# Reading the moving columns of fp32r products last to first, and moving the weight tiles by steps of 32 bytes

## The chip, the cores and the metric

The kernel runs on one core of a Trainium2 chip. The time is the device time of one execution in microseconds (us); a version is judged by its median over several executions. The profile comes from one execution of its own.

## The reference

Two transformer blocks follow each other on 256 tokens of width 2048, all in float32. The first has banded attention and gated linear attention, the second block attention and retention; each then has a gated feed-forward part of width 5632 and a gated embedding. Nearly all the arithmetic is in products with large weight matrices:

```python
def first_block(x, p, ...):
    h = rms_norm(x, norm_mix_w);  proj = h @ w_in                    # 2048 x 6160
    ...                                                              # attention, gated linear attention
    x = x + concat([y_a, y_g]) @ w_out                               # 2048 x 2048
    u = causal_depthwise_conv(rms_norm(x, norm_ffn_w) @ w_ffn_up)    # 2048 x 11264
    x = x + (gelu(u_gate) * u_val) @ w_ffn_down                      # 5632 x 2048
    x = x + sigmoid(rms_norm(x, norm_ple_w) @ w_ple_gate) * (p @ w_ple_proj)
    return rms_norm(x, final_norm_w)
# second_block: w_in_2 2048 x 7168, w_o_2, w_gate_2 and w_up_2 2048 x 5632, w_down_2, w_ple_gate_2, w_ple_proj_2
```

## The kernel before

**Products in parts.** Each float32 operand is split into a high part, rounded to fp32r by a copy, and a low part, the rest. A product is made of three: high times high, high times low and low times high. `weight_plan` (line 29) cuts all weights into 880 tiles of 128 partitions x up to 1024 numbers, in the order in which they are used. Tiles follow each other in *chunks*, the tiles that belong to the same output columns.

**Narrow chunks** (`prod_b`, line 276): 256 output columns, four k-steps in a tile, 4, 5 or 6 tiles in a chunk. The weights stand still (128 x 128) and the activations move. For each k-step and each half `b` of the output there is a pair of products: the high weights against 512 columns (high and low part of the activations, side by side), and the low weights against the 256 columns of the high part. The plan has 172 narrow chunks: 140 of 4 tiles, 16 of 6 and 16 of 5, together 736 tiles, and a tile has 8 pairs.

**Wide chunks** (`prod_a`, line 289): up to 512 output columns, two k-steps in a tile, 8 tiles in a chunk. Here the activations stand still and the weights move: 12 products a tile. The plan has 17 of them: 15 are 512 columns wide, the second is 256 and the third 272. Eight further tiles, the embedding's, go through `prod_p` (line 267), 24 products of 256 columns each.

**Where a weight tile lies.** `load` (line 178) fetches a tile by DMA seven tiles ahead, ScalarE writes its high part four ahead (`split_hi`, line 188), VectorE its low part three ahead (`split_lo`, line 196). Each of the two parts has its own buffers of 4096 + 256 bytes, aligned to 256 bytes, and `split_tile` (line 170) chooses how many bytes into the buffer the part begins. `PARTS_AT` gives this for the high and the low part: `narrow` 192 and 0, `lead` 0 and 32, `wide` 0 and 0. `plan_kind` calls the first two tiles of every eighth narrow chunk (n mod 8 = 0) and the first tile where n mod 8 = 4 `lead`: 65 tiles in all. The activations lie in regions aligned to 256 bytes.

**Order.** The order of the instructions is written out by hand: a tile's `slot` (line 207) issues the splits and the load for later tiles and a step of the pending evictions and side work, then come the products of the tile. All matmuls of these kinds go through `mm` (line 259), so the profile shows them on line 260, and the accumulators are called `acc`. Two accumulators of two PSUM banks alternate.

Of the kernel before, what the change touches and what calls it, by code (L numbers as in the profile page):

```python
# [13 lines left out]
T = 256  # L14
# [7 lines left out]
HALVES = ((0, 24), (24, 44))  # L22
LINE = 256
SCRATCH = 2048
LEADS = {0: 2, 4: 1}
PARTS_AT = {"narrow": (192, 0), "lead": (0, 32), "wide": (0, 0)}


def weight_plan():

    tiles = []
    full = tuple(range(KT))

    def gemm(n, kts, chunks):
        for ch in chunks:
            for i in range(0, len(kts), n):  # L40
                tiles.append((kts[i : i + n], ch))

    def even(name, lo, hi, step):
        return [[(name, c, c + step)] for c in range(lo, hi, step)]

    def wide(name, lo, hi):
        gemm(2, full, even(name, lo, hi, 512))

    def narrow(name, lo, hi, kts=full):
        gemm(4, kts, even(name, lo, hi, 256))  # L50

    def ffn(gate, up, off, down):
        for a, b in HALVES:
            gemm(4, full, [[(gate, c * P, c * P + P), (up, off + c * P, off + c * P + P)] for c in range(a, b)])
            narrow(down, 0, D, tuple(range(a, b)))

    def ple(gate, proj):
        for c in range(0, D, 512):
            narrow(gate, c, c + 512)
            gemm(2, (0, 1), even(proj, c, c + 512, 512))  # L60

    gemm(2, full, [[("w_in", 4096, 4608)], [("w_in", 4608, 4864)], [("w_in", 4864, 5120), ("w_in", 6144, 6160)]])
    narrow("w_in", 3072, 4096)
    narrow("w_in", 0, 2048)
    wide("w_in", 2048, 3072)
    wide("w_in", 5120, 6144)
    narrow("w_out", 0, D, MIX_ORDER)
    ffn("w_ffn_up", "w_ffn_up", FF, "w_ffn_down")
    ple("w_ple_gate", "w_ple_proj")
    wide("w_in_2", 0, 3072)  # L70
    narrow("w_in_2", 3072, 5120)
    wide("w_in_2", 5120, 7168)
    narrow("w_o_2", 0, D)
    ffn("w_gate_2", "w_up_2", 0, "w_down_2")
    ple("w_ple_gate_2", "w_ple_proj_2")
    return tiles


def plan_offsets(tiles):
    out, off = [], 0  # L80
    for kts, ch in tiles:
        f = len(kts) * sum(b - a for _, a, b in ch)
        out.append((off, f))
        off += P * f
    return out, off


def plan_kind(tiles):

    out, last, n, k = [], None, -1, 0  # L90
    for kts, ch in tiles:
        if ch != last:
            n, k = n + (len(kts) == 4), 0
        out.append("wide" if len(kts) == 2 else "lead" if k < LEADS.get(n % 8, 0) else "narrow")
        k += 1
        last = ch
    return out

# [15 lines left out]
class Net:  # L114
# [4 lines left out]
    def __init__(self, nc, tc, pools, ins, out):  # L119
        self.nc, self.tc = nc, tc  # L120
        self.sp, self.wp, self.ps = pools
        self.ins, self.out = ins, out
        self.plan = weight_plan()
        self.offs, _ = plan_offsets(self.plan)
        self.kind = plan_kind(self.plan)
        self.i = 0
        self.raw, self.H, self.L = {}, {}, {}
        self.ev, self.side = [], []
        self.done = set()
        self.nacc = 0  # L130
        self.forced = []
        self.sizes = {}
        self.off = SCRATCH + 128
        self.pad(self.wp)
        self.off += 4 * 4096 + 9 * (4096 + LINE)
# [32 lines left out]


    def split_tile(self, i, tag, bufs):  # L170
        o = PARTS_AT[self.kind[i]][tag == "wl"] // 4
        return self.wp.tile([P, 1024 + LINE // 4], F32R, tag=tag, name=tag, bufs=bufs)[:, o : o + 1024]

    def cut(self, i, part):
# [101 lines left out]
    def prod_b(self, acts, acc):  # L276
        nk = len(acts)
        for g in range(0, nk, 4):
            self.need_acts(acts[g : g + 4])
            H, L, w = self.slot(4)  # L280
            assert w == 256
            for j in range(4):
                x, _ = acts[g + j]
                for b in range(2):
                    sl = slice(j * w + b * P, j * w + b * P + P)
                    self.mm(acc[:, b, :], H[:, sl], x, g + j == 0, False)
                    self.mm(acc[:, b, T:], L[:, sl], x[:, :T], False, g + j == nk - 1)

    def prod_a(self, acts, acc):
        nk = len(acts)  # L290
        for g in range(0, nk, 2):
            self.need_acts(acts[g : g + 2])
            H, L, w = self.slot(2)
            for j in range(2):
                x, _ = acts[g + j]
                for t in range(2):
                    o = acc[:, t, :w]
                    hs = slice(t * P, t * P + P)
                    ls = slice(T + t * P, T + t * P + P)
                    sl = slice(j * w, j * w + w)  # L300
                    self.mm(o, x[:, hs], H[:, sl], g + j == 0, False)
                    self.mm(o, x[:, hs], L[:, sl], False, False)
                    self.mm(o, x[:, ls], H[:, sl], False, g + j == nk - 1)

    def join(self, acc, dst):

# [1113 lines left out]
```

## Time and profile before

| what | value |
|---|---|
| median of 3 runs | 2477.26 us (2477.2 to 2477.84) |
| profiled execution | 2477.44 us, its span 2475.6 us |
| TensorE busy | 2464.0 us, 14162 matmuls |
| VectorE, ScalarE busy | 1667.6 us, 1279.5 us |
| read from HBM | 464.80 MB, 189 GB/s over the span |

A matmul's row gives its start, and a modelled length that overlaps the next matmul. What a product costs is therefore read from the distance between starts. A weight load stands beside the product before it, on a row of its own (PEld). In the timeline `acc<-f,wh` is a product of the activations `f` with the high part of a weight tile, `acc<-f,wl` with the low part.

### The profile page before, as it was taken

The numbers are of one execution on the slowest core, as the hardware profiler recorded it, in microseconds if no ns is written. First come the engines' busy times: TensorE is split into PE (matmuls) and PEld (weight loads), VectorE is DVE, ScalarE is ACT, GpSimd is POOL, SyncE is SP. The second block draws the span as 40 slices with busy tenths as digits, with TensorE's granted clock in tenths as the row PEclk, the third lists the DMA queues.
The fourth block names the chain that finished last, engine by engine and source line by source line (L and its number), as shares of the span: only waits on it lengthen the run. The fifth ranks groups of instructions, "written<-read, shape, count | busy, mean of one in ns | idle before, by whom it ended". The sixth has DMA issues, their size and how long they took to land.

```text
span 2475.6 us, 36486 instructions
## 1 busy us (share of the span) xinstructions
PE 2464.0 (100%) x14162; PEld 2153.4 (87%) x14162; DVE 1667.6 (67%) x2374; ACT 1279.5 (52%) x1713; POOL 8.4 (0%) x60
## 2 busy tenths in 40 slices
PE   9999999999999999999999999999999999999999
PEld 7888788888888888888888888888888888888888
DVE  6666667777755787767886765676666556666665
ACT  6545655665633565545644644555554434554453
POOL 0000000000000000000000000000000000000000
PEclk9999999999999999999999999999999999999999
DMA  7545455555555555555555455555555555555554
GB/s 245 190 145 192 155 190 188 195 194 192 193 195 192 192 195 195 195 199 192 198 179 187 162 183 188 182 193 191 195 192 192 195 195 193 191 195 198 191 201 147
DMA packets 133550, 469.30 MB, mean 190 GB/s; under 512 B 14960, under 2 KB 17392, under 8 KB 133376
## 3 DMA queue, kind: packets, MB, share of 16 engines
q1 hardware_dynamic: 133232, 466.95, 56.5%
q8 instruction: 111, 1.82, 0.3%
q14 instruction: 63, 0.52, 0.1%
q10 hardware_dynamic: 144, 0.01, 0.0%
HBM read 464.80 MB, written 2.10 MB: 189 GB/s over the span
## 4 chain that ended last, share of the span: by engine, by line
PE 99%; DMA 0%; DVE 0%; ACT 0%; issue 0%; SPq 0%; ACTq 0%
PE acc L260 95%; PE sc L260 2%; PE pv L260 1%; PE tr L698 0%; DMA raw<-weights 0%; PE sc L1147 0%; ACT wh L194 0%; PE sc L1230 0%; PE sc L566 0%; DVE ty L996 0%; SPq L428 0%; DVE wl L205 0%; DVE X L997 0%; PE tr L785 0%; SPq L186 0%
## 5 line engine op out<-in xcount | busy, mean ns | idle before, releaser
L205 DVE TENSOR_TENSOR wl<-raw,wh 128x1024 fp32r<-128x1024 f32 (+1 forms) x881 | 1069.0, 1214 | 761.8 <-PE acc L260 492.9
L194 ACT ACTIVATE wh<-raw 128x1024 fp32r<-128x1024 f32 (+1 forms) x881 | 925.6, 1051 | 844.9 <-PE acc L260 665.6
L260 PE MATMUL acc<-f,wh 128*128 128x512 f32 x2816 | 960.0, 390 | 0.0
L260 PE MATMUL acc<-f,wl 128*128 128x256 f32 x2816 | 777.7, 276 | 0.0
L260 PEld LDWEIGHTS acc<-f,wh 128*128 128x128 f32 x2816 | 528.6, 188 | 110.5
L260 PEld LDWEIGHTS acc<-f,wl 128*128 128x128 f32 x2816 | 528.6, 188 | 0.0
L260 PE MATMUL acc<-g,wh 128*128 128x512 f32 x1408 | 479.6, 389 | 0.0
L260 PE MATMUL acc<-g,wl 128*128 128x256 f32 x1408 | 388.8, 276 | 0.0
L260 PEld LDWEIGHTS acc<-g,wh 128*128 128x128 f32 x1408 | 264.3, 188 | 55.5
L260 PEld LDWEIGHTS acc<-g,wl 128*128 128x128 f32 x1408 | 264.3, 188 | 0.0
L260 PE MATMUL acc<-hp,wh 128*128 128x512 f32 x512 | 175.5, 390 | 0.0
L260 PE MATMUL acc<-hp,wl 128*128 128x256 f32 x512 | 141.5, 276 | 0.0
L260 PEld LDWEIGHTS acc<-hp,wh 128*128 128x128 f32 x512 | 96.1, 188 | 19.9
L260 PE MATMUL acc<-wh,m2b 128*128 128x512 f32 x320 | 102.8, 393 | 0.0
L260 PE MATMUL acc<-wh,m2a 128*128 128x512 f32 x320 | 102.3, 392 | 0.0
L260 PEld LDWEIGHTS acc<-hp,wl 128*128 128x128 f32 x512 | 96.1, 188 | 0.0
L897 ACT ACTIVATE ty<-tU,vec 128x256 f32<-128x256 f32 x88 | 48.3, 596 | 74.4 <-DVE tU L893 74.4
L308 ACT ACTIVATE tq<-acc 128x512 f32<-128x512 f32 x124 | 71.8, 579 | 4.7 <-PE acc L260 4.7
L260 PE MATMUL acc<-wh,h0a 128*128 128x512 f32 (+2 forms) x224 | 67.1, 376 | 4.7 <-ACT wh L194 4.7
L260 PEld LDWEIGHTS acc<-wh,m2a 128*128 128x128 f32 x320 | 60.1, 188 | 12.3
L260 PEld LDWEIGHTS acc<-wh,m2b 128*128 128x128 f32 x320 | 60.1, 188 | 12.2
L260 PE MATMUL acc<-h0a,wh 128*128 128x512 f32 x192 | 67.6, 395 | 0.0
(272 smaller groups left out, 2746.9 us busy)
## 6 DMA issues: line engine op xcount, KB each, us to landing
raw<-weights SPq DMA_DIRECT2D x863, 512.0 KB, 3.3
raw<-weights SPq DMA_DIRECT2D x10, 256.0 KB, 3.3
raw<-weights SPq DMA_DIRECT2D x8, 272.0 KB, 2.8
aB<-bias SPq DMA_DIRECT2D x8, 256.0 KB, 3.5
X<-xT SPq DMA_DIRECT2D x7, 256.0 KB, 7.1
dk<-decay SPq DMA_DIRECT2D x8, 192.0 KB, 3.7
out<-X SPq DMA_DIRECT2D x6, 256.0 KB, 2.8
pr<-pT SPq DMA_DIRECT2D x2, 256.0 KB, 4.9
```

The costliest lines, as they stand in the source:

```text
L194: self.nc.scalar.activation(self.H[i][:, a], self.raw[i][:, a], AF.Copy)
L205: self.nc.vector.tensor_sub(self.L[i][:, a], r[:, a], self.H[i][:, a].bitcast(F32))
L260: self.nc.tensor.matmul(out, lhsT, rhs, start=start, stop=stop, skip_group_check=True, **kw)
L308: self.nc.scalar.activation(m, acc[:, :, T:], AF.Copy)
L897: nc.scalar.activation(y[:, b, :], u[:, b, 0:T], AF.Identity, scale=self.col("cw0", j), bias=self.col("b_ffn_conv", j))
```

## The change

The table of places with its three kinds goes. A narrow tile's high part now begins 32 x (n mod 8) bytes into its buffer and its low part 32 x ((n // 8 + n) mod 8), with n the number of the narrow chunk; wide tiles stay at 0 and 0. In narrow chunks both products of a pair take their moving columns from the last to the first and write the sums from the last to the first, so that every sum lands where it did. In wide chunks the 2nd, 4th, ... 16th do the same and the others stay as they were.

```diff
--- before.py
+++ after.py
@@ -22,8 +22,6 @@
 HALVES = ((0, 24), (24, 44))
 LINE = 256
 SCRATCH = 2048
-LEADS = {0: 2, 4: 1}
-PARTS_AT = {"narrow": (192, 0), "lead": (0, 32), "wide": (0, 0)}
 
 
 def weight_plan():
@@ -85,14 +83,12 @@
     return out, off
 
 
-def plan_kind(tiles):
-
-    out, last, n, k = [], None, -1, 0
+def plan_places(tiles):
+
+    out, last, n = [], None, -1
     for kts, ch in tiles:
-        if ch != last:
-            n, k = n + (len(kts) == 4), 0
-        out.append("wide" if len(kts) == 2 else "lead" if k < LEADS.get(n % 8, 0) else "narrow")
-        k += 1
+        n += len(kts) == 4 and ch != last
+        out.append((32 * (n % 8), 32 * ((n // 8 + n) % 8)) if len(kts) == 4 else (0, 0))
         last = ch
     return out
 
@@ -122,7 +118,8 @@
         self.ins, self.out = ins, out
         self.plan = weight_plan()
         self.offs, _ = plan_offsets(self.plan)
-        self.kind = plan_kind(self.plan)
+        self.places = plan_places(self.plan)
+        self.nwide = 0
         self.i = 0
         self.raw, self.H, self.L = {}, {}, {}
         self.ev, self.side = [], []
@@ -168,7 +165,7 @@
 
 
     def split_tile(self, i, tag, bufs):
-        o = PARTS_AT[self.kind[i]][tag == "wl"] // 4
+        o = self.places[i][tag == "wl"] // 4
         return self.wp.tile([P, 1024 + LINE // 4], F32R, tag=tag, name=tag, bufs=bufs)[:, o : o + 1024]
 
     def cut(self, i, part):
@@ -283,11 +280,13 @@
                 x, _ = acts[g + j]
                 for b in range(2):
                     sl = slice(j * w + b * P, j * w + b * P + P)
-                    self.mm(acc[:, b, :], H[:, sl], x, g + j == 0, False)
-                    self.mm(acc[:, b, T:], L[:, sl], x[:, :T], False, g + j == nk - 1)
+                    self.mm(acc[:, b, ::-1], H[:, sl], x[:, ::-1], g + j == 0, False)
+                    self.mm(acc[:, b, T:][:, ::-1], L[:, sl], x[:, :T][:, ::-1], False, g + j == nk - 1)
 
     def prod_a(self, acts, acc):
         nk = len(acts)
+        self.nwide += 1
+        d = 1 if self.nwide % 2 else -1
         for g in range(0, nk, 2):
             self.need_acts(acts[g : g + 2])
             H, L, w = self.slot(2)
@@ -298,9 +297,9 @@
                     hs = slice(t * P, t * P + P)
                     ls = slice(T + t * P, T + t * P + P)
                     sl = slice(j * w, j * w + w)
-                    self.mm(o, x[:, hs], H[:, sl], g + j == 0, False)
-                    self.mm(o, x[:, hs], L[:, sl], False, False)
-                    self.mm(o, x[:, ls], H[:, sl], False, g + j == nk - 1)
+                    self.mm(o[:, ::d], x[:, hs], H[:, sl][:, ::d], g + j == 0, False)
+                    self.mm(o[:, ::d], x[:, hs], L[:, sl][:, ::d], False, False)
+                    self.mm(o[:, ::d], x[:, ls], H[:, sl][:, ::d], False, g + j == nk - 1)
 
     def join(self, acc, dst):
```

## Rows read from the trace of the kernel before

**Rows 1.** Page: span, busy times, and the chain that ended last.

```profile
span 2475.6 us, 36486 instructions
...
PE 2464.0 (100%) x14162; PEld 2153.4 (87%) x14162; DVE 1667.6 (67%) x2374; ACT 1279.5 (52%) x1713; POOL 8.4 (0%) x60
...
PE 99%; DMA 0%; DVE 0%; ACT 0%; issue 0%; SPq 0%; ACTq 0%
```

**Rows 2.** Waits of TensorE: total us, times, longest us.

```profile
PE acc L260 <- ACT wh L194: 4.7, 1, 4.7
PE pv L260 <- ACT rfb L381: 1.0, 1, 1.0
PE acc L260 <- DVE wl L205: 0.7, 1, 0.7
```

**Rows 3.** Chain of waits in order of time: start, length (us), what.

```profile
422.35 713.90 PE acc L260 x4192
1150.95 21.76 PE acc L260 x128
...
1224.95 24.51 PE acc L260 x108
...
1394.91 5.60 PE acc L260 x32
...
1667.93 713.84 PE acc L260 x4192
```

**Rows 4.** Stretches: length, busy time by engine, granted clock, DMA share, GB/s.

```profile
328.00:1136.00 808.00, 808.00 (x4750) 714.72 (x4749) 579.14 (x764) 439.14 (x567) 4.35 (x42) 1.00 0.58 194
```

**Rows 5.** Timeline of TensorE, chunk 24: start, length; lines 16 pairs apart.

```profile
449.42 0.40 PE L260 MATMUL acc<-f,wh 128*128 128x512 f32 x1
...
454.96 0.39 PE L260 MATMUL acc<-f,wh 128*128 128x512 f32 x1
...
460.40 0.39 PE L260 MATMUL acc<-f,wh 128*128 128x512 f32 x1
```

**Rows 6.** Timeline of TensorE, chunk 11: lines eight pairs apart.

```profile
195.27 0.40 PE L260 MATMUL acc<-h0a,wh 128*128 128x512 f32 x1
...
198.07 0.40 PE L260 MATMUL acc<-h0a,wh 128*128 128x512 f32 x1
```

**Rows 7.** Timeline, embedding products of 256 columns: lines 21 products apart.

```profile
1148.15 0.28 PE L260 MATMUL sc<-ph,wl 128*128 128x256 f32 x1
...
1150.67 0.28 PE L260 MATMUL sc<-ph,wl 128*128 128x256 f32 x1
```

**Rows 8.** Timeline, a wide chunk after small products: lines nine products apart.

```profile
1520.62 0.39 PE L260 MATMUL acc<-wl,m2b 128*128 128x512 f32 x1
...
1522.69 0.39 PE L260 MATMUL acc<-wl,m2b 128*128 128x512 f32 x1
```

**Rows 9.** Groups of VectorE and ScalarE in one narrow chunk, 438.5 to 449.4 us.

```profile
L205 DVE TENSOR_TENSOR wl<-raw,wh 128x1024 fp32r<-128x1024 f32 x4 | 4.9, 1225 | 2.2 <-issue 1.2 <-ACT g L877 0.8 <-PE acc L260 0.2
L194 ACT ACTIVATE wh<-raw 128x1024 fp32r<-128x1024 f32 x4 | 4.2, 1060 | 1.4 <-issue 1.2 <-PE acc L260 0.3
```

**Rows 10.** Stretch at the start, columns as in rows 4.

```profile
8.60:12.00 3.40, 3.00 (x7) 1.70 (x6) 1.81 (x4) 2.31 (x5) 0.00 (x0) 1.00 1.03 410
```

## The prediction

> **What bounds the kernel now.** I read the page first: TensorE is busy for the whole span and the chain that ended last lies on it for 99%, nearly all on one helper line, the matmul call [rows 1]. Then the waits of TensorE: three in all, 6.4 us together, all at the start or in norms [rows 2]. So nothing feeds TensorE too late, and the time is the number of products times their pace. The pace is not in the "mean ns" column, since ends are modelled and products overlap. It is in the start times, and the chain's long unbroken pieces give it best [rows 3]: 4192 products in 713.90 us are 2096 pairs (512 columns with the high part, 256 with the low part) at 340.6 ns each; the second half gives the same.
>
> The reader is to see three things there. First, 768 columns at the granted 2.4 GHz (the clock column reads 1.00, [rows 4]) would be 320 ns, so a pair loses 20 ns, one part in 16, though nobody is waited for. Second, the pace depends on where the weight tile lies: in a chunk with `lead` tiles 16 pairs take 454.96 - 449.42 = 5.54 us, 346 ns each, and the next 16 pairs of the same chunk, same operands, weights 192 and 0 bytes in, take 460.40 - 454.96 = 5.44 us, 340 ns [rows 5]. Third, it depends on history: at 195 us eight pairs with the very same places take 198.07 - 195.27 = 2.80 us, 350 ns [rows 6], and this lasts until other products break in; the piece of 32 products in 5.60 us in the second block is the same pace [rows 3]. So there are a few steady paces, as if the moving read and the weight load beside it settled into one of several alignments, each with its own number of lost cycles. Both parts of the change touch exactly this.
>
> **The change part by part.**
>
> *Count of what it touches.* From the plan: 736 narrow tiles of 8 pairs are 5888 pairs, all reversed. Of 17 wide chunks the 2nd, 4th, ... 16th are reversed, 8 chunks of 96 products; one of them is 256 columns wide, so 672 products of 512 columns turn.
>
> *Lead tiles go.* 65 tiles x 8 pairs x (346.6 - 340.0) ns = 3.4 us less. This is the difference between 340.6 in the long pieces and 340.0 in a piece without lead tiles, 128 products in 21.76 us [rows 3], and it is contained in the sum below.
>
> *New places of both parts.* The high part lies at 32 x (n mod 8), the low part at 32 x ((n/8 + n) mod 8), so 64 combinations come in turn over 172 chunks, among them the pair (0, 32) that was slow and ones like the present pair. The trace shows two combinations only, and three steady paces: 340.0, 346.6 and 350.0 ns. I take their plain mean, 345.5 ns, for a mix of combinations, because none of the three is known to be usual; the ends are 340.0 and 350.0.
>
> *Descending columns.* No product of before reads or writes backwards, so no row prices it. Bounds: nothing (the same number of columns, the same addresses, one instruction each), up to the pace of the plain 256-column products of the embedding, 2.52 us for 21 products, 120 ns each [rows 7], where the present pair spends 113 on its 256 columns; below nothing it can go as far as the 20 ns that a pair now loses. Averaged over all alignments, two regular streams meet equally often whichever way one of them runs; direction alters which alignment is settled into. So I put it at nothing beyond the mix of paces above.
>
> *Reversed wide products.* Undisturbed they take 24.51 us for 108, 227 ns [rows 3]; after an interruption they take 1522.69 - 1520.62 = 2.07 us for nine, 230 ns [rows 8]. Between 0 and +3 ns each, 672 x 1.5 ns = 1 us.
>
> *The writers of the tiles.* ACT and VectorE write the same elements, at other offsets inside the same padded buffer: 1060 and 1225 ns of a 2.72 us tile [rows 9]. Both engines have gaps, and loads run at 0.58 of the DMA share [rows 4]; they cost nothing. If the cover were gone one would see TensorE waiting on them, as it does once now [rows 2]. A pace of 2.56 us a tile would ask for 205 GB/s, and the start shows 410 [rows 10], so a gain would not be stopped by loads.
>
> *Sum.* Profiled run 2477.44 us: span 2475.6 and 1.84 around it; the median, 2477.26, is 0.2 us less, which I leave out. Narrow: 5888 x (345.5 - 340.6) ns = +28.9 us. Wide: +1. Total 2507 us. With the ends: 340.0 gives -3.5 us, 2474; 350.0 and 3 ns on the wide ones give +55 + 2, 2535.
>
> *The skill against the trace.* Rows 5 show a tile's byte place costing 6 ns a pair. The Trainium skill, "SBUF — State Buffer", section "SBUF: two separate sides", says that of the engine ports only the pair shared by VectorE and GpSimd contends and that TensorE never waits on anyone; by that rule the place costs nothing and the change is worth the lead tiles at most. The trace does not agree as far as TensorE's own two reads go. The Trainium skill, "PSUM — Partial Sum Buffer", section "Specifications (TRN2)", speaks against the change: it gives PSUM 8-byte lines and says that any non-contiguous pattern slows matmuls significantly. No product of before shows whether a step of -1 counts as contiguous.
>
> **The rivals.**
>
> *Reversal breaks the loss (faster).* If the 20 ns of a pair come from moving read and weight load walking the same way through the same lines, a descending read could pass the load instead of following it. Half of the loss gone: 5888 x (340.6 - 330) = 62 us, wide 672 x 6.7 ns = 4.5 us, 2411 us; all of it gone: 2347. For it: the loss is there and moves with places and history [rows 5, 6]. Against it: 340 = 320 x 17/16 in the narrow chunks and 227 = 213 x 17/16 in the wide ones, so the best pace looks like a floor that does not ask who the operands are. It decides as soon as the mean over the 64 combinations falls under 340.6.
>
> *Every place settles at 340 (same).* Then only the lead tiles go: 2474 us, -0.14%. For it: wide chunks, at (0, 0), find back to 227 within a tile. Against: rows 5 and 6.
>
> *More meetings (much slower).* If descending, the load's lines are met each time, as the 120 ns of rows 7 may already be: 120 + 240 = 360 ns a pair, 5888 x 19.4 = +114 us, wide 672 x 13.3 = +9, 2600 us.
>
> *Descending pairs break a line.* If two neighbouring sums no longer share one write, a product would take twice as long: 5888 x 340 ns = +2002 us, 4480 us. The rule of the skill on PSUM lines above is this case.
>
> **How the numbers follow.** About 0.2%, 5 us, is what a measurement can tell from no change. Forecast, a mix of paces between 340 and 350, 2474 to 2535: 0.48, of which 0.02 lies within 5 us. Reversal breaks the loss: 0.23. All at 340: 0.10. More meetings: 0.12. Broken lines: 0.07. Faster 0.23, same 0.12, slower 0.65. The likeliest is 2507 us. For 8 in 10 I keep the forecast, the 340 case, the nearer half of the faster case down to 2400 and the 360 ns case up to 2600; left out are the broken lines and the far half of the gain.
>
> **What would show it.** In the narrow chunks, spacing of starts chunk by chunk: my forecast wants paces that change with n and come back 64 chunks later, between 340 and 353. All chunks at 340 is the second rival, all near 360 the third, any long stretch under 340 the first. The wide chunks are a test inside one run: forward and reversed ones at the same place (0, 0); equal spacing, 227, says that direction costs nothing. New waits of TensorE on ACT or VectorE would mean the cover was misjudged. A direction effect of its own, of either sign, over 5 ns a pair makes the forecast wrong.

## The result, and the profile after

The changed kernel takes 2550.59 us (median, 2549.92 to 2551.14) against 2477.55 us for the kernel before on the same chip: ratio 1.0292, 95% interval 1.0281 to 1.0304, that is 73 us slower. The forecast was 2507 us, 30 us slower. Direction right, size less than half of what came.

Little else in the profile moved. The page of the changed kernel has the same number of instructions, the chain again lies on the matmul call (now line 257), and TensorE waits three times, as in [rows 1, 2]:

```profile
span 2548.1 us, 36486 instructions
...
PE 2536.6 (100%) x14162; PEld 2182.2 (86%) x14162; DVE 1667.8 (65%) x2374; ACT 1278.5 (50%) x1713; POOL 8.4 (0%) x60
...
PE 99%; DMA 0%; DVE 0%; ACT 0%; issue 0%; SPq 0%; ACTq 0%
```

Waits of TensorE in the changed kernel (total us, times, longest us):

```profile
PE acc L257 <- ACT wh L191: 4.5, 1, 4.5
PE pv L257 <- ACT rfb L380: 1.0, 1, 1.0
PE acc L257 <- DVE wl L202: 0.8, 1, 0.8
```

The granted clock is 1.00 in the long stretch, as in [rows 4], so the clock is not what changed. The time is in the pace. Its chain in order of time (start, length in us, what), beside [rows 3]:

```profile
429.11 739.52 PE acc L257 x4192
1183.63 22.61 PE acc L257 x128
...
1711.95 739.58 PE acc L257 x4192
```

The same 2096 pairs now take 739.52 us instead of 713.90, 352.8 ns a pair instead of 340.6. Over 5888 pairs 12.2 ns would be 72 us. The chunks in which the kernel before already ran at 350 ns [rows 6] give less, and the wide products add a little. In the timeline of TensorE two chunks of 32 pairs follow each other, with places (96, 192) and (128, 224):

```profile
490.94 0.40 PE L257 MATMUL acc<-f,wh 128*128 128x512 f32 x1
...
502.19 0.40 PE L257 MATMUL acc<-f,wh 128*128 128x512 f32 x1
...
513.70 0.40 PE L257 MATMUL acc<-f,wh 128*128 128x512 f32 x1
```

The first takes 11.25 us, 352 ns a pair, the second 11.51 us, 360 ns. This second place is the only one of the 64 that stands out: in the chunks that no other product interrupts, all the others run at 351 to 355 ns. So the mix of paces that I had expected from the places is hardly there; a raised floor is.

The wide chunks are the test inside the run. A reversed one and the forward one after it (timeline of TensorE, lines three products apart):

```profile
1260.03 0.40 PE L257 MATMUL acc<-wl,m2a 128*128 128x512 f32 x1
...
1260.73 0.40 PE L257 MATMUL acc<-wl,m2a 128*128 128x512 f32 x1
...
1261.43 0.40 PE L257 MATMUL acc<-wl,m2a 128*128 128x512 f32 x1
...
1283.12 0.39 PE L257 MATMUL acc<-wl,m2a 128*128 128x512 f32 x1
...
1283.80 0.39 PE L257 MATMUL acc<-wl,m2a 128*128 128x512 f32 x1
...
1284.48 0.39 PE L257 MATMUL acc<-wl,m2a 128*128 128x512 f32 x1
```

Reversed: 0.70 us for three, 233 ns each. Forward: 0.68 us, 227 ns, as before [rows 3]. Weights and activations lie at the same byte places in both, so direction alone costs 6 ns a product here.

### The profile page after: what moved, and what is told of

Its sections match the earlier page's. It is cut to its first block, busy times and chain, and to the rows that moved or that the text cites. A ratio compares the mean times of both kernels' runs of the same rounds, so it can differ in the third digit from the quotient of the medians.

```text
span 2548.1 us, 36486 instructions
## 1 busy us (share of the span) xinstructions
PE 2536.6 (100%) x14162; PEld 2182.2 (86%) x14162; DVE 1667.8 (65%) x2374; ACT 1278.5 (50%) x1713; POOL 8.4 (0%) x60
## 4 chain that ended last, share of the span: by engine, by line
PE 99%; DMA 0%; DVE 0%; ACT 0%; issue 0%; SPq 0%; ACTq 0%
PE acc L257 95%; PE sc L257 2%; PE pv L257 1%; PE tr L697 0%; DMA raw<-weights 0%; PE sc L1146 0%; ACT wh L191 0%; PE sc L1229 0%; PE sc L565 0%; DVE ty L995 0%; SPq L427 0%; DVE wl L202 0%; DVE X L996 0%; PE tr L784 0%; SPq L183 0%
## 5 line engine op out<-in xcount | busy, mean ns | idle before, releaser
L257 PE MATMUL acc<-f,wh 128*128 128x512 f32 x2816 | 994.3, 398 | 0.0
L257 PE MATMUL acc<-f,wl 128*128 128x256 f32 x2816 | 792.2, 281 | 0.0
L257 PE MATMUL acc<-g,wh 128*128 128x512 f32 x1408 | 497.0, 398 | 0.0
L257 PE MATMUL acc<-g,wl 128*128 128x256 f32 x1408 | 396.0, 281 | 0.0
L257 PE MATMUL acc<-hp,wh 128*128 128x512 f32 x512 | 181.5, 398 | 0.0
```

The costliest lines, as they stand in the source:

```text
L257: self.nc.tensor.matmul(out, lhsT, rhs, start=start, stop=stop, skip_group_check=True, **kw)
```

## Experiments

All are edits of the kernel before unless said otherwise. Where a run turns only the narrow products, the wide ones stay as before. Of each edit a line or two that carry it are shown; where one product of a pair is shown, the other is edited alike. A time without a range beside it is that of a single execution. For each the line of the chain is shown that answers to the 713.90 us of [rows 3]: the same 2096 pairs, with no other product between them.

### Which half of the change, and which side of the product

*Places alone*: the changed kernel with both product functions as before.

```diff
-                    self.mm(acc[:, b, ::-1], H[:, sl], x[:, ::-1], g + j == 0, False)
+                    self.mm(acc[:, b, :], H[:, sl], x, g + j == 0, False)
```

> The changed kernel with the moving columns and the sums running first to last again, so only the byte places of the weight parts vary by chunk and the lead tiles are gone. Direction theory (the changed kernel's 351 to 353 ns a pair come from the descending order alone): every chunk runs at about 340 ns a pair whatever its place, time about 2474 us, the lead tiles' 3.4 us less than before. Places theory (the forecast's mix of paces): paces between 340 and 350 ns that change with the place, mean near 345, time about 2505 us. If the places were all of the loss: 2550 us.

Measured: 2526.12 us (2525.84 to 2526.35), ratio 1.0193, interval 1.0176 to 1.0210.

```profile
427.17 732.49 PE acc L257 x4192
```

349.5 ns a pair. Places do cost in a forward walk, 349.5 ns where I had taken 345.5, but alone they are not the whole of the 73 us. At the places (64, 0) eight pairs take 2.82 us at one point of the run (from 778.49 us) and 2.72 us at another (from 1791.86 us), 353 against 340 ns. The activations there are `g` in one case and `f` in the other, so this does not show by itself that the pace depends on what ran before; the run without lead tiles, at the end, does.

*Direction alone*: the two product functions of the changed kernel, places and lead tiles as before.

```diff
-                    self.mm(acc[:, b, :], H[:, sl], x, g + j == 0, False)
+                    self.mm(acc[:, b, ::-1], H[:, sl], x[:, ::-1], g + j == 0, False)
```

> The kernel before, with only the direction turned (all narrow products, every second wide chunk); places 192 and 0, lead tiles 0 and 32, as before. Direction theory: 351 to 353 ns a pair in ordinary narrow tiles, reversed wide products 233 ns, time 2543 to 2553 us. Places theory: about 340 ns a pair, time about 2480 us.

Measured: 2544.21 us (2544.11 to 2544.67), ratio 1.0266, interval 1.0251 to 1.0282.

```profile
428.73 737.40 PE acc L261 x4192
```

351.8 ns a pair. The halves are +49 and +67 us, together +73: they do not add. A reversed walk has its own pace, little moved by the places, which replaces the paces of the forward one.

*Only the read reversed*, and *only the write reversed*, in all narrow and every second wide chunk:

```diff
+                    self.mm(acc[:, b, :], H[:, sl], x[:, ::-1], g + j == 0, False)      # read
+                    self.mm(acc[:, b, ::-1], H[:, sl], x, g + j == 0, False)            # write
```

> As e2, but the sums are written first to last, so only the read of the moving columns descends; the sums land in mirrored columns, so the values are others, while number, size and order of all instructions stay. Read theory (the descending moving read meets the weight load's read more often): as e2, 351 to 353 ns a pair, about 2550 us. Write theory (descending sums cost in PSUM): as before, 340 ns a pair, about 2478 us.

Measured: 2544.64 us.

```profile
429.26 737.40 PE acc L261 x4192
```

> As e2, but the moving columns are read first to last and only the sums are written last to first; the sums land in mirrored columns, so the values are others. Read theory: 340 ns a pair, about 2478 us. Write theory: 351 to 353 ns a pair, about 2550 us. If both sides cost: something between in e3 and in e4, adding up to 73 us.

Measured: 2477.42 us.

```profile
422.32 713.90 PE acc L261 x4192
```

To the hundredth of a microsecond, in this stretch, the read is the whole of it and the write is free.

### Is it the weight load that the read meets?

My theory at this point was that the lost cycles come from the weight load and the moving read meeting in memory. Two pairs of runs vary the load: 64 columns instead of 128, and one column read 128 times.

```diff
+                    m = P if g + j == 0 else P // 2
+                    self.mm(acc[:m, b, :], H[:, sl][:, :m], x, g + j == 0, False)       # e7; e8 with ::-1
+                    self.mm(acc[:, b, :], H[:, sl.start : sl.start + 1].broadcast_to([P, P]), x, g + j == 0, False)  # e5; e6 with ::-1
```

> The kernel before, but every narrow product except the first k-step of a chunk loads and uses only 64 of its 128 weight columns (half of the outputs is left out); number and order of instructions and the 512 and 256 moving columns stay. Meeting theory (the lost cycles of a pair come from the weight load's read meeting the moving read): half as much load, so about half of the 20 ns is lost, 330 ns a pair instead of 340, time about 2420 us. Floor theory (17/16 belongs to the moving read alone): 340 ns a pair still, 2475 us.

Measured: 2481.54 us.

```profile
422.43 715.84 PE acc L260 x4192
```

> As e7 with the narrow products reversed (wide ones not). Meeting theory: the 32 ns that a reversed pair loses fall to about 16, 336 ns a pair, about 6 ns more than in e7, time about 2455 us. Floor theory with a dearer descending read: 352 ns a pair still, time about 2540 us, 12 ns a pair over e7.

Measured: 2537.06 us.

```profile
427.77 736.11 PE acc L260 x4192
```

Half the load leaves 341.5 ns forward and 351.2 ns reversed. Its rows fall from 188 ns each to 133 to 135:

```profile
L260 PEld LDWEIGHTS acc<-f,wh 128*64 128x64 f32 x2640 | 351.7, 133 | 243.2
```

Lost cycles in proportion to the load are refuted.

> The kernel before, but every narrow product loads one weight column 128 times over (step 0), so the load reads one address and sweeps nothing; the values are others. Meeting theory: the pace no longer depends on place or history, every pair in ordinary and lead tiles the same; if the repeated read stays out of the way, 320 to 330 ns a pair, time 2360 to 2420 us. Floor theory: 340 ns a pair, about 2475 us.

Measured: 2512.94 us.

```profile
426.13 726.73 PE acc L260 x4192
```

> As e5 with the narrow products reversed (wide ones not). Meeting theory: equal to e5 within 2 ns a pair, since a load that sweeps no addresses has no direction. Floor theory with a dearer descending read: 12 ns a pair, some 70 us, more than e5.

Measured: 2538.32 us.

```profile
429.45 735.93 PE acc L260 x4192
```

346.7 ns forward, 351.1 ns reversed. Neither expectation holds in either run: forward, the repeated load is slower than the ordinary one instead of equal or faster, and the difference that direction makes, 4.4 ns, is neither under 2 nor 12. It shrinks because the forward pace rises. The reversed pace hardly moves with the load, 351.8, 351.2 and 351.1 ns. So how much a load reads does not set the reversed pace; that the load plays no part at all is not shown, since its place and a repeated column do move the forward pace.

### What about the read costs?

*One moving column, 512 or 256 times over:*

```diff
+                    self.mm(acc[:, b, :], H[:, sl], x[:, 0:1].broadcast_to([P, 512]), g + j == 0, False)
+                    self.mm(acc[:, b, T:], L[:, sl], x[:, 0:1].broadcast_to([P, T]), False, g + j == nk - 1)
```

> The kernel before; every narrow product reads one moving column 512 or 256 times over (step 0), so values are others. If the 20 ns that the best pair loses belong to walking through memory with the moving read: 320 to 326 ns a pair, 2360 to 2400 us. If they belong to the stream of products itself, whatever it reads: 340 ns, about 2475 us.

Measured: 2413.93 us.

```profile
414.71 691.68 PE acc L260 x4192
```

330.0 ns a pair, in lead tiles and ordinary ones alike. Of the 20 ns that the best pair loses, 10 belong to walking through memory and 10 remain without it. The 17/16 that I had called a floor is half made by the walk.

*Order of 16-byte groups against order inside them*: the same columns in groups of four, groups from the last to the first (e10), or last to first only inside a group (e11). Groups of 16 and of 64 columns, from the last to the first and upwards inside, follow (e13, e14), then every second group of four upwards and the others after it (e15).

```diff
+  x.rearrange("p (a b) -> p a b", b=4)[:, ::-1, :]      # e10; b=16: e13, b=64: e14
+  x.rearrange("p (a b) -> p a b", b=4)[:, :, ::-1]      # e11
+  x.rearrange("p (g s c) -> p s g c", s=2, c=4)         # e15, and the sums written alike
```

> The kernel before; narrow products read their moving columns in groups of four (16 bytes) from the last group to the first, first to last inside a group; sums are written first to last, so values are others. If the cost of descending lies in the order of 16-byte groups: 351 to 352 ns a pair as in e3, about 2543 us. If it lies inside a group: 340 ns, about 2478 us. If neither, the price of a read in pieces shows, above 353 ns.

Measured: 2540.63 us.

```profile
428.22 737.40 PE acc L260 x4192
```

> The mirror of e10: groups of four first to last, last to first inside a group. If the order inside a group costs: 351 to 352 ns a pair, about 2543 us; if the order of the groups does: 340 ns, about 2478 us.

Measured: 2477.25 us.

```profile
422.20 713.90 PE acc L260 x4192
```

Groups backwards is the reversed pace exactly; backwards inside a group is the pace of before exactly. The cost lies in the order of the 16-byte groups. Both runs have a two-part pattern with a step backwards in it, so the form of the instruction is not what costs.

> As e10, but the groups that are taken from the last to the first are 16 columns (64 bytes) long, read upwards inside; sums written first to last, values are others. If each step to a lower group costs: a quarter of e10's 12 ns, 343 ns a pair, about 2493 us. If only the direction over longer distances counts: 351 ns as in e10, 2540 us.

Measured: 2578.89 us.

```profile
430.78 753.33 PE acc L260 x4192
```

> As e13 with blocks of 64 columns (256 bytes). If each step to a lower group costs: a sixteenth, 341 ns a pair, about 2480 us. If the direction over longer distances counts: 351 ns, 2540 us.

Measured: 2477.37 us.

```profile
422.30 713.90 PE acc L260 x4192
```

> The kernel before; narrow products read every second 16-byte group of their moving columns upwards, then the other ones upwards, and write the sums in the same order to where they belong, so the result is the reference's. If only descending costs: 340 ns a pair, 2477 us. If any order but the plain walk upwards costs: 345 to 353 ns, 2505 to 2550 us. If the 10 ns that a walk costs over one standing column come from neighbouring groups: under 340 ns, 2420 to 2470 us.

Measured: 2541.18 us.

```profile
425.95 739.97 PE acc L260 x4192
```

Blocks of 64 bytes taken backwards are the worst of all, 359.4 ns, outside both expectations, though three of four steps go up: it is not a fixed price per step down. Blocks of 256 bytes backwards cost nothing, 340.6 ns: a walk that goes up inside each 256 bytes is as good as one that goes up throughout. Every second group, upwards, 353.0 ns: an order may cost though no step but one goes down. (In this run the sums too are written every second 16 bytes; that a write in pieces is free was shown for a step of -1 alone, so the share of the write stays open here.) So the order of the 16-byte groups counts within short distances and, by the 256-byte blocks, not between blocks of that length; no order tried beats the plain walk upwards. Blocks of 128 bytes were not tried, nor whether the 256-byte blocks are free for their length or because so few steps go down.

### A version slightly faster than both

*No lead tiles*: all narrow tiles at 192 and 0, forward.

```diff
-LEADS = {0: 2, 4: 1}
+LEADS = {}
```

> The kernel before without lead tiles: all narrow tiles at 192 and 0, first to last. If the lead tiles are mere cost: 340 ns a pair everywhere, 3.4 us less, 2474 us. If they bring the stream back to 340 ns after side work has left it at 350: long stretches at 350, up to 58 us more for all 5888 pairs, between 2480 and 2530 us.

Measured: 2472.85 us (2472.46 to 2476.17), ratio 0.9983, interval 0.9973 to 0.9993.

```profile
422.37 712.67 PE acc L260 x4192
```

340.0 ns throughout the long pieces. The lead tiles are mere cost in this kernel, 4.5 us by the medians. That is 0.2%, about the least that I had said a measurement can tell, but the trace shows where it goes: about 3.4 us are the lead tiles themselves (1.23 us in this stretch, beside [rows 3]), and 1.0 us is history. The eight pairs of [rows 6], in chunk 11, took 2.80 us before; here the same pairs take 2.72:

```profile
195.77 0.39 PE L260 MATMUL acc<-h0a,wh 128*128 128x512 f32 x1
...
198.49 0.39 PE L260 MATMUL acc<-h0a,wh 128*128 128x512 f32 x1
```

Chunks 9 to 11 have no lead tile in either kernel; operands, places and code are the same. They run at 350.0 ns a pair before and at 340.0 here, 96 pairs by 10 ns. Only earlier lead tiles differ, the last of them in chunk 8, with two ordinary tiles behind it. So the pace of a whole chunk does depend on what ran earlier.

## Why the prediction was wrong

**The bound: right.** TensorE's pace and nothing else; no wait grew by more than 0.1 us, the loads and both writers of the tiles stayed hidden at 353 ns a pair.

**Lead tiles, 3.4 us: right**, shown by taking them away alone; the further 1.0 us, the slower chunks that they left behind, was not in the forecast.

**Descending columns, put at nothing: the step that failed.** The argument was that two regular streams meet equally often whichever way one runs, averaged over alignments, so only the mix of paces would change. The direction alone costs 351.8 - 340.6 = 11.2 ns a pair. Two things in the argument were wrong. The halved load shows that the loss does not shrink with the load's reads, so an average over meetings says nothing about it. And the order of the groups matters by itself, as the runs in blocks show. So even the upper end of the sum, 2535 us, fell short. The upper bound that stood beside it, 120 ns for 256 columns, that is 360 ns a pair and 2600 us, held; the measured pace lies between the two. That the change came out slower, as forecast, is in large part luck: reversal, put at nothing, gives 67 of the 73 us alone.

**Places, mean of three paces, 345.5 ns: mis-sized.** Alone they give 349.5 ns, +8.9 a pair instead of +4.9, and 49 us instead of 29. I took three paces with equal weight; in the trace of the places alone 340 is the rare one (three of the 154 chunks that nothing interrupts), and 346 to 354 are usual. The best pace had been found by choice of one place, so a sample made of that place and one other said little of the other 62.

**The sum of the two: not tried in the forecast.** Had I had both terms right, 8.9 and 11.2 ns, adding them would have given 118 us. They replace each other: reversed, the places move the pace by less than 4 ns but for one.

**Reversed wide products, 0 to 3 ns: mis-sized**, 6 ns each. The row I had taken, after an interruption, was no measure of direction.

**The rivals.** Reversal breaks the loss: fell. All at 340: fell, both halves cost. More meetings, 360 ns: the sign was right; in the changed kernel the price was reached at one place only, and the mechanism as I put it, the load's lines met more often, is refuted by the halved load. Broken lines in PSUM: refuted, since the write alone is free. The Trainium skill, "PSUM — Partial Sum Buffer", section "Specifications (TRN2)", says that any non-contiguous pattern slows matmuls significantly; a step of -1 does not fall under it here, 713.90 us in either case. The Trainium skill, "SBUF — State Buffer", section "Specifications (TRN2)", gives SBUF 16-byte lines and a penalty for each cross to a new line. That order inside 16 bytes is free agrees with it, 713.90 us in either case; but the groups backwards cross to a new line no more often than forwards and still cost 11 ns a pair.

**What stays open.** Why the order of the groups costs, and whether the moving read meets anything at all. Shown are that 256-byte blocks backwards are free and 64-byte blocks are not, an effect of the weight tile's place, memory of earlier work and a loss that does not shrink with half a load; the mechanism that joins them is not.

## What to carry to other kernels

When products run back to back without a wait, take their price from the distance of starts, and treat the order in which the moving operand is read as part of it: upwards inside each 256 bytes was best here, and writing sums backwards was free. A pace that was tuned by choosing one place says nothing of other places; before forecasting a mix, measure more than the chosen one. An order of access for which no row exists deserves a range that is not centred on zero by an argument of symmetry, and two effects on one pace need not add.

## What the runs showed of the hardware that was not expected

- A pair of fp32r products (512 and 256 columns) takes 330.0 ns with one standing moving column, 340.0 walking upwards (340.6 with the lead tiles among them, as in all that follow), 351.8 with the 16-byte groups backwards, 353.0 with every second group, 359.4 with 64-byte blocks backwards, and 340.6 with 256-byte blocks backwards.
- Half the weight columns loaded do not make a pair faster: 341.5 ns against 340.6.
- With the same code, places and operands a forward stream ran three whole chunks at 340.0 or at 350.0 ns, depending on the lead tiles that had run before; reversed, the chunks that nothing interrupts kept to 351 to 355 at all places but one, where they took 360.
